# Seven block products instead of eight for a quad of weight tiles in the last FFN

## Chip, cores and metric

The kernel runs on one core of a Trainium2 chip. The metric is the device time of one execution in microseconds; the median of several runs is quoted. Five engines work side by side, each with its own in-order queue: TensorE (PE in the profile, its weight loads PEld), VectorE (DVE), ScalarE (ACT), GpSimd (POOL) and SyncE (SP, which here only issues DMAs).

## What is computed

One residual block on 256 tokens of width 2048 in float32: an FFN, a mixer (mLSTM and RG-LRU side by side), and a second FFN. The change touches the second FFN:

```python
def _swiglu(u, w13, w2):
    g, v = jnp.split(u @ w13, 2, axis=-1)
    return (jax.nn.silu(g) * v) @ w2

y = _swiglu(modulate(x, 2), ffn2_w13[l], ffn2_w2[l])
x = _layer_norm(ALPHA * x + FFN_WEIGHT * gate[:, 2, None, :] * y, ln_g[l, 2], ln_b[l, 2])
```

`w13` is 2048 x 11264 (5632 gate columns and 5632 value columns), `w2` is 5632 x 2048. `gate` comes from a product of the conditioning vector c with `w_ada`.

## The kernel before

**Precision.** A float32 product is made of three products in the PE's faster type: both operands are split into a high part `hi` and a rest `lo`, and hi*hi, hi*lo and lo*hi are summed in PSUM. For the tokens these are `uh` and `ul`. For a weight tile (128 x 2048: four chunks of 128 rows by 512 columns), `load` (line 83) fetches 1 MB into a buffer of the tag "raw" (four of them), `split` (line 90) has ACT cast it into a `hi` buffer (line 97) and DVE subtract to get `lo` (line 99); there are three buffers of each.

**The product of a tile.** `mov_t` (line 264) multiplies a tile with one half t of the tokens (128 of 256): 4 chunks x 3 matmuls (lines 271 to 273) with the tokens as stationary and 512 weight columns as moving operand, 12 matmuls in all. `mov_w` (line 296) does both halves, 24 matmuls.

**The last FFN.** The 5632 hidden columns are 11 blocks b of 512; two blocks are a group gi. `rows_block(b)` (line 648) takes 4 gate tiles and 4 value tiles (the k-th covers 512 of the 2048 input rows), and `swiglu` (line 667) makes silu(g)*v. `turn_one` (line 674) transposes such a 128 x 512 piece with four PE instructions, ACT and DVE split it into `hth` and `htl`. `g2(gi)` (line 862) multiplies a group with its 8 tiles of w2 and adds into `yacc`. The loop at the end of `ffn` runs block 0 and 1, blocks 2 and 3, g2(0), blocks 4 and 5, g2(1) and so on to blocks 8 and 9, g2(3), then `residual` (line 309) on what has been summed, block 10, and `closing` (line 897) with the last three sets of w2 tiles and the last LayerNorm.

**Work in between.** The rows of `w_ada` are reduced on DVE by `ada_tile` (line 181): a load into a raw buffer and one multiply-and-sum with `scb`, silu(c) in every partition. `tick` (line 199) is called by every load, adds `credit[1]` (here FFN2_RATE, from a start of -2) and issues an ada tile whenever a whole credit has gathered. `gate_rows` (line 206) turns the finished gate column into a row and spreads it over the partitions by DMA on POOL's queue. `scale_x` (line 318) multiplies x by ALPHA on ACT.

**What sets the order.** A planner orders each engine's instructions ahead of time by its own timing; on each engine it takes what it thinks is ready, the earlier written first, and buffers are given out as they come free. Only instructions issued through `Pinned` handles (line 113: V, A, G, T, Q) keep the written order among themselves. In the last FFN before the change the weights' products are not pinned.

Of the kernel before, what the change touches and what calls it, by code (L numbers as in the profile page):

```python
# [29 lines left out]
GRP = 8  # L30
# [8 lines left out]
RAMP_RATE = (1.0, 0.8, 1.0, 0.6)  # L39
FFN1_RATE = 0.88  # L40
MIX_RATE = 0.5
FFN2_RATE = 0.3

SLOT = 2176


@with_exitstack
def block_kernel(ctx: ExitStack, tc: tile.TileContext, a: dict, out: bass.AP):
    nc = tc.nc
# [15 lines left out]
    def bank(name):  # L65
        return psp.tile([P, 512], F32, tag="ps", name=name)
# [4 lines left out]
    def raw_tile(name):  # L71
        n_raw[0] += wide[0]
        if wide[0] and n_raw[0] % 3 == 0:
            return slot(name)[:, 0:D]
        return wp.tile([P, 2048], F32, tag="raw", bufs=4, name=name)


    credit = [0.0, 0.0]
# [34 lines left out]
    class Pinned:  # L113


        def __init__(self, engine):
            self.engine = engine
            self.last = None
# [36 lines left out]
            T.matmul(ps[:, 0:P], ident, ident, start=True, stop=True)  # L155


    scb = big.tile([P, D], F32, name="scb")
    sc = cst.tile([P, KT], F32, name="sc")
    nc.scalar.dma_start(sc, a["c"])  # L160
    nc.scalar.activation(sc, sc, AF.Silu)
# [1 line left out]
    idle(c_rows[3], 9)  # L163
    for n in range(4):
        rows_of(c_rows[n], sc[:, 4 * n:4 * n + 4])
    x = big.tile([P, NT, D], F32, name="x")


    u2 = big.tile([P, KT, 2, S], F32R, name="u2")
    uh, ul = u2[:, :, 0, :], u2[:, :, 1, :]  # L170
# [1 line left out]
    badac = cst.tile([P, 3, 3, KT], F32, name="badac")  # L172
    adac = cst.tile([P, 3, 3, KT], F32, name="adac")
    modc = adac[:, :, 0:2, :]
    gate = big.tile([P, D], F32, name="gate")
    rowd = ctx.enter_context(tc.tile_pool(name="dr", bufs=1, space=bass.MemoryType.DRAM)).tile([KT, P], F32, name="rowd")


    todo = list(enumerate(_ada_tiles()))
# [26 lines left out]
    def gate_rows(s, weight):  # L206

        ps = bank(f"adag{s}")
        nc.tensor.transpose(ps[0:KT, 0:P], adac[:, s, 2, :], ident)
        row = sm.tile([KT, P], F32, tag="grow", bufs=1, name=f"grow{s}")  # L210
        nc.scalar.mul(row, ps[0:KT, 0:P], weight)
        nc.gpsimd.dma_start(rowd, row)
        nc.gpsimd.dma_start(gate, rowd.rearrange("a b -> (a b)").rearrange("(o n) -> o n", o=1).to_broadcast([P, D]))


    def rstd_of(var, name):
# [44 lines left out]
        for k in range(KT):  # L261
            nc.tensor.matmul(ps[:, 0:S], lo[:, k * P:(k + 1) * P], uh[:, k, :], start=False, stop=k == KT - 1)  # L262

    def mov_t(ps, hl, acth, actl, k0, t, first, last):

        hi, lo = hl
        tk = slice(t * P, (t + 1) * P)
        for j in range(4):
            w = slice(j * 512, (j + 1) * 512)
            o = like(ps, hi)  # L270
            nc.tensor.matmul(o, acth[:, k0 + j, tk], cut(hi, w), start=first and j == 0, stop=False)  # L271
            nc.tensor.matmul(o, acth[:, k0 + j, tk], cut(lo, w), start=False, stop=False)  # L272
            end = nc.tensor.matmul(o, actl[:, k0 + j, tk], cut(hi, w), start=False, stop=last and j == 3)  # L273
        return end

    def mov_u(ps, hl, k, t, first, last, between=lambda: None, both=True):
# [16 lines left out]
            w = slice(j * 512, (j + 1) * 512)  # L293
            T.matmul(o, ul[:, 4 * k + j, t * P:(t + 1) * P], cut(hl[0], w), start=False, stop=last and j == 3)

    def mov_w(pss, hl, acth, actl, k0, first, last):
        for t in range(NT):
            end = mov_t(pss[t], hl, acth, actl, k0, t, first, last)
        return end

    def half(t):
# [16 lines left out]
    def scale_x():  # L318
        for t in range(NT):
            A.mul(x[:, t, :], x[:, t, :], ALPHA)  # L320
# [312 lines left out]
    def ffn(s, w13, w2, start, following=None):  # L633
# [11 lines left out]
        def new_h(gi):  # L645
            hts[gi] = [slot(f"{w}{gi}", F32R)[:, 0:GRP * S].rearrange("p (a b) -> p a b", a=GRP) for w in ("hth", "htl")]

        def rows_block(b, passed=None):

            i = 8 * (b - b0)  # L650
            if passed:
                pg, pv = passed[0], met(passed, w13[4:8], f"fv{s}")
            else:
                pg = [bank(f"fg{s}{b}{t}") for t in range(NT)]
                for k in range(4):
                    end = mov_w(pg, load_w(w13[i + k], f"fg{s}_{b}{k}"), uh, ul, k * 4, k == 0, k == 3)
                    if k in (1, 2):
                        turn_one(end)
                pv = [bank(f"fv{s}{b}{t}") for t in range(NT)]
                for k in range(4):  # L660
                    mov_w(pv, load_w(w13[i + 4 + k], f"fv{s}_{b}{k}"), uh, ul, k * 4, k == 0, k == 3)
            if 4 * b // GRP not in hts:
                new_h(4 * b // GRP)
            for t in range(NT):
                swiglu(b, t, pg[t], pv[t])

        def swiglu(b, t, g, v):

            sg = sm.tile([P, 512], F32, tag="u", bufs=2, name=f"sg{s}{b}{t}")
            nc.scalar.activation(sg, g, AF.Silu)  # L670
            nc.vector.tensor_mul(sg, sg, v)
            to_turn.append((b, t, sg))
# [261 lines left out]
        if start is not None:  # L934
            ramp(start)
            credit[:] = 0.0, FFN1_RATE
            done = 2
            g2(0)
        else:
            credit[:] = -2.0, FFN2_RATE  # L940
            rows_block(0, nxt.pop())
        for gi in range(done, len(groups)):
            g1(gi)
            if gi == 2 and not start:
                scale_x()
            if gi == len(groups) - 2:
                ada_until(s, 2, KT - 1)
                gate_rows(s, 0.5)
                credit[0] -= 2.0
            if gi == len(groups) - 1 and following:  # L950
                credit[:] = 0.0, 0.0
                g2_kept(gi - 1)
            elif gi == len(groups) - 1:
                closing(gi)
            elif gi:
                g2(gi - 1)
# [467 lines left out]
```

## Time and profile before

| | us |
|---|---|
| median of 3 runs (1895.41 to 1895.69) | 1895.65 |
| span of the profiled execution | 1893.8 |
| PE busy in it | 1880.4 |
| DVE busy | 1411.9 |
| ACT busy | 831.2 |
| POOL busy | 41.3 |
| read from HBM | 512.36 MB, 272 GB/s |

The profile is that of one execution. A matmul's end is modelled and neighbouring matmuls overlap, so the distance between two starts tells more than a duration. "Idle before" of a group names what ended the idle time of its engine. The profiled execution is 1.85 us shorter from first to last instruction than the median run; the rest lies around the instructions.

### The profile page before, as it was taken

The numbers are of one execution on the slowest core, as the hardware profiler recorded it, in microseconds if no ns is written. First come the engines' busy times: TensorE is split into PE (matmuls) and PEld (weight loads), VectorE is DVE, ScalarE is ACT, GpSimd is POOL, SyncE is SP. The second block draws the span as 40 slices with busy tenths as digits, with TensorE's granted clock in tenths as the row PEclk, the third lists the DMA queues.
The fourth block names the chain that finished last, engine by engine and source line by source line (L and its number), as shares of the span: only waits on it lengthen the run. The fifth ranks groups of instructions, "written<-read, shape, count | busy, mean of one in ns | idle before, by whom it ended". The sixth has DMA issues, their size and how long they took to land.

```text
span 1893.8 us, 21255 instructions
## 1 busy us (share of the span) xinstructions
PE 1880.4 (99%) x8591; PEld 1544.5 (82%) x8591; DVE 1411.9 (75%) x1372; ACT 831.2 (44%) x790; POOL 41.3 (2%) x65
## 2 busy tenths in 40 slices
PE   9999999999999999999999999999999999999998
PEld 6788888888888888788888887888888888888886
DVE  6899998887887977798986877556555644545666
ACT  4443444533334335756643357343434334343341
POOL 0000000000000000000000121000000000000000
PEclk9999999999999999999999999999999999999999
DMA  9989889899899886477787663666676655555562
GB/s 378 416 355 360 311 315 374 336 354 351 344 362 356 333 316 252 170 289 269 274 320 269 215 248 128 242 257 248 239 258 242 227 196 193 184 200 202 198 222 89
DMA packets 74498, 515.87 MB, mean 272 GB/s; under 512 B 8688, under 2 KB 8864, under 8 KB 13472
## 3 DMA queue, kind: packets, MB, share of 16 engines
q1 hardware_dynamic: 72144, 507.54, 71.3%
q10 hardware_dynamic: 1728, 3.80, 0.6%
q0 software_dynamic: 528, 3.17, 0.4%
q8 instruction: 67, 1.10, 0.2%
q14 instruction: 31, 0.25, 0.0%
HBM read 512.36 MB, written 2.12 MB: 272 GB/s over the span
## 4 chain that ended last, share of the span: by engine, by line
PE 94%; DVE 3%; DMA 1%; ACT 1%; issue 1%; POOL 0%; POOLq 0%; DVEq 0%; SPq 0%; ACTq 0%
PE py L272 6%; PE py L271 6%; PE py L273 6%; PE fg L272 6%; PE fg L271 6%; PE fg L273 6%; PE fv L271 6%; PE fv L272 6%; PE fv L273 6%; PE pj L260 5%; PE pj L262 3%; PE tl L271 2%; PE tl L272 2%; PE tl L273 2%; PE rv L738 2%; PE rv L739 2%
## 5 line engine op out<-in xcount | busy, mean ns | idle before, releaser
L191 DVE CUSTOM_DVE_ANT_0 ada<-ada,scb,badac 128x2048 f32<-128x2048 f32 x110 | 258.0, 2346 | 11.3 <-DMA ada<-in_w_ada 10.9
L99 DVE TENSOR_TENSOR lw<-rw,hw 128x2048 fp32r<-128x2048 f32 x81 | 185.3, 2290 | 96.2 <-ACT hw L97 96.2
L97 ACT CAST hw<-rw 128x2048 fp32r<-128x2048 f32 x81 | 155.1, 1914 | 216.9 <-PE py L273 80.8
L99 DVE TENSOR_TENSOR lfv<-rfv,hfv 128x2048 fp32r<-128x2048 f32 x60 | 137.5, 2292 | 133.9 <-ACT hfv L97 133.7
L99 DVE TENSOR_TENSOR lfg<-rfg,hfg 128x2048 fp32r<-128x2048 f32 x60 | 137.5, 2291 | 89.7 <-ACT hfg L97 89.6
L272 PE MATMUL py<-lw,hth 128*128 128x512 f32 x512 | 199.4, 389 | 0.1
L273 PE MATMUL py<-hw,htl 128*128 128x512 f32 x512 | 199.4, 389 | 0.0
L97 ACT CAST hfg<-rfg 128x2048 fp32r<-128x2048 f32 x60 | 114.9, 1914 | 191.4 <-PE fv L273 52.9
L271 PE MATMUL py<-hw,hth 128*128 128x512 f32 x512 | 197.7, 392 | 0.0
L97 ACT CAST hfv<-rfv 128x2048 fp32r<-128x2048 f32 x60 | 114.6, 1912 | 165.3 <-PE fg L273 91.7
L272 PE MATMUL fg<-lfg,u 128*128 128x512 f32 x480 | 187.0, 389 | 0.1
L273 PE MATMUL fg<-hfg,u 128*128 128x512 f32 x480 | 187.0, 389 | 0.0
L272 PE MATMUL fv<-lfv,u 128*128 128x512 f32 x480 | 186.8, 389 | 0.0
L273 PE MATMUL fv<-hfv,u 128*128 128x512 f32 x480 | 186.7, 389 | 0.0
L271 PE MATMUL fg<-hfg,u 128*128 128x512 f32 x480 | 185.0, 392 | 0.0
L271 PE MATMUL fv<-hfv,u 128*128 128x512 f32 x480 | 183.5, 389 | 0.0
L260 PE MATMUL pj<-u,hs 128*128 128x512 f32 x512 | 122.5, 391 | 0.0
L97 ACT CAST hra<-rra 128x2048 fp32r<-128x2048 f32 x38 | 72.6, 1915 | 102.8 <-DMA rra<-in_w_r 49.1
L272 PEld LDWEIGHTS py<-lw,hth 128*128 128x128 f32 x512 | 96.2, 188 | 20.4 <-DVE lw L99 0.9
L273 PEld LDWEIGHTS py<-hw,htl 128*128 128x128 f32 x512 | 96.1, 188 | 20.2
L271 PEld LDWEIGHTS py<-hw,hth 128*128 128x128 f32 x512 | 95.9, 188 | 19.3
L260 PEld LDWEIGHTS pj<-u,hs 128*128 128x128 f32 x512 | 94.3, 188 | 18.4
(472 smaller groups left out, 3552.5 us busy)
## 6 DMA issues: line engine op xcount, KB each, us to landing
ada<-in_w_ada SPq DMA_DIRECT2D x138, 1024.0 KB, 6.0
rw<-in_w SPq DMA_DIRECT2D x81, 1024.0 KB, 5.0
rfg<-in_w SPq DMA_DIRECT2D x60, 1024.0 KB, 4.8
rfv<-in_w SPq DMA_DIRECT2D x60, 1024.0 KB, 4.8
rra<-in_w_r SPq DMA_DIRECT2D x45, 1024.0 KB, 7.4
rs<-in_w_s SPq DMA_DIRECT2D x32, 1024.0 KB, 4.9
rwo<-in_w_out SPq DMA_DIRECT2D x16, 1024.0 KB, 4.8
rv<-in_w_vo SPq DMA_DIRECT2D x8, 1024.0 KB, 4.9
```

What stands on the lines that cost most here:

```text
L97: act.copy(cut(hi, w), like(raw[:, w], hi))
L99: low.tensor_sub(cut(lo, w), like(raw[:, w], lo), cut(hi, w).bitcast(F32))
L191: vec.tensor_tensor_reduce(raw[:, c], raw[:, c], scb[:, c], 1.0, base, ALU.mult, ALU.add, to)
L260: nc.tensor.matmul(ps, hi[:, k * P:(k + 1) * P], both(k), start=k == 0, stop=False)
L262: nc.tensor.matmul(ps[:, 0:S], lo[:, k * P:(k + 1) * P], uh[:, k, :], start=False, stop=k == KT - 1)
L271: nc.tensor.matmul(o, acth[:, k0 + j, tk], cut(hi, w), start=first and j == 0, stop=False)
L272: nc.tensor.matmul(o, acth[:, k0 + j, tk], cut(lo, w), start=False, stop=False)
L273: end = nc.tensor.matmul(o, actl[:, k0 + j, tk], cut(hi, w), start=False, stop=last and j == 3)
L738: pe.matmul(pss[t], uh[:, k0 + j, tk], hi[:, w], start=go, stop=False)
L739: pe.matmul(pss[t], uh[:, k0 + j, tk], lo[:, w], start=False, stop=False)
```

## The change

For blocks 2 to 9, `rows_block` and `g2` are replaced by `fast_block`. It takes the gate tiles 0 and 1 (ta, tb) and the value tiles 0 and 1 (tc_, td), a 2 x 2 quad with the token halves on the other side, by Strassen's scheme in Winograd's form: 7 calls of `mov_t` for the quad, not 8. Four of them use sums of token blocks, which `sums` makes once into `ws`; the weight sums are made in place in the raw buffers, four subtractions of a whole tile on DVE a block, and the results are split like tiles. The other four w13 tiles are multiplied as before, 8 calls. Partial results are copied out of PSUM by ACT (`kept`) and added by DVE. Four w2 tiles are written in between in each block (`x_tile`), for the group two blocks earlier. All these products go through T, so PE keeps the written order.

`ws` takes the place of x in SBUF: x goes to DRAM (`xd`) before the first of these blocks and comes back after the last. Two more raw buffers (six) replace the own places of `scb` and `gate`, which now hold one raw buffer each as long as they live. FFN2_RATE becomes 0.5. `mov_t` and `mov_w` get the engine handle as an argument. `scale_x` moves from group 2 to behind the way back of x.

The core of the diff (left out: the handle arguments, small helpers, and the loop over groups, which skips what `fast_block` has done):

```diff
-FFN2_RATE = 0.3
+FFN2_RATE = 0.5
+RAW = 6
+FAST = range(2, 10)
+class Held:
+    def __init__(self, tile):
+        self.tile = tile
+    def __getitem__(self, key):
+        return self.tile[key]
...
-        return wp.tile([P, 2048], F32, tag="raw", bufs=4, name=name)
+        return wp.tile([P, 2048], F32, tag="raw", bufs=RAW, name=name)
-    scb = big.tile([P, D], F32, name="scb")
+    scb = raw_tile("scb")
-    x = big.tile([P, NT, D], F32, name="x")
+    def tokens(name):
+        return big.tile([P, NT, D], F32, tag="x", name=name)
+    x = Held(tokens("x0"))
-    gate = big.tile([P, D], F32, name="gate")
+    gate = Held(raw_tile("gate0"))
+    xd = dr.tile([P, NT, D], F32, name="xd")
...
+        def sums():
+            nc.gpsimd.dma_start(xd, x.tile)
+            f = raw_tile("sums").rearrange("p (a b) -> p a b", b=P)
+            for t in range(NT):
+                tk = slice(t * P, (t + 1) * P)
+                nc.vector.tensor_add(f[:, 8 * t:8 * t + 8, :], uh[:, 0:8, tk].bitcast(F32), ul[:, 0:8, tk].bitcast(F32))
+            a11, a12, a21, a22 = (f[:, 4 * i:4 * i + 4, :] for i in range(4))
+            nc.vector.tensor_add(a22, a21, a22)
+            nc.vector.tensor_sub(a21, a11, a21)
+            nc.vector.tensor_sub(a11, a22, a11)
+            nc.vector.tensor_sub(a12, a12, a11)
+            both = big.tile([P, 2, KT, P], F32R, tag="x", name="ws")
+            nc.scalar.copy(both[:, 0], f)
+            nc.vector.tensor_sub(both[:, 1], f, both[:, 0].bitcast(F32))
+            return both[:, 0], both[:, 1]
+        def restore():
+            x.tile = tokens("x1")
+            for t in range(NT):
+                nc.gpsimd.dma_start(x[:, t, :], xd[:, t, :])
+            scale_x()
+        def fast_block(b, wh, wl):
...
+            u, w = (uh, ul), (wh, wl)
+            ta = fresh(0)
+            end = part(p1, halves(ta), u, 0, 0, True, True)
+            turn_one(end)
+            f1 = kept(p1, "u", "fs")
+            tc_ = fresh(4)
+            end = x_tile(0)
+            turn_one(end)
+            nc.vector.tensor_sub(ta[0], tc_[0], ta[0])
+            part(p5, halves(ta, "p"), w, s1_, 0, True, True)
+            f5 = kept(p5, "gy", "ft")
+            td = fresh(5)
+            x_tile(1)
+            nc.vector.tensor_sub(ta[0], td[0], ta[0])
+            part(p1, halves(ta, "q"), w, s2_, 0, False, True)
+            f2 = kept(p1, "gy", "fv")
+            part(p5, halves(td), w, s4_, 0, False, False)
+            x_tile(2)
+            nc.vector.tensor_sub(tc_[0], td[0], tc_[0])
+            part(p1, halves(tc_, "q"), w, s3_, 0, False, True)
+            f3 = kept(p1, "u", "fu")
+            p2, p4 = bank(f"fc{b}"), bank(f"fd{b}")
+            tb = fresh(1)
+            part(p2, halves(tb), u, 4, 0, True, False)
+            g2_ = load_w(w13[i + 2], f"fw{s}_{b}2")
+            part(p2, g2_, u, 8, 0, False, False)
+            part(p4, g2_, u, 8, 1, True, False)
+            nc.vector.tensor_sub(tb[0], tb[0], ta[0])
+            part(p4, halves(tb, "p"), u, 4, 1, False, False)
+            g3_ = load_w(w13[i + 3], f"fw{s}_{b}3")
+            part(p2, g3_, u, 12, 0, False, True)
+            part(p4, g3_, u, 12, 1, False, True)
+            nc.vector.tensor_add(f1, f1, p2)
+            nc.scalar.activation(f1, f1, AF.Silu)
+            nc.vector.tensor_add(f3, f3, p4)
+            nc.scalar.activation(f3, f3, AF.Silu)
+            x_tile(3)
+            vs = [load_w(w13[i + 4 + k], f"fw{s}_{b}{4 + k}") for k in (2, 3)]
+            for t, ps in enumerate((p5, p1)):
+                for k in range(2):
+                    part(ps, vs[k], u, 8 + 4 * k, t, False, k == 1)
...
+            for t, h, v, ps in ((0, f1, f2, p5), (1, f3, f5, p1)):
+                nc.vector.tensor_add(v, v, ps)
+                nc.vector.tensor_mul(h, h, v)
+                to_turn.append((b, t, h))
...
             rows_block(0, nxt.pop())
+            rows_block(1)
+            ws = sums()
+            for b in FAST:
+                fast_block(b, *ws)
+            restore()
+            done = FAST.stop // 2 - 1
```

In the parts left out, `fresh(k)` is a load of w13 tile k, `halves` is split on ACT and DVE, `part` is mov_t with T, `kept` copies a PSUM bank to SBUF on ACT, and `x_tile(m)` is load_w and mov_w of one w2 tile with the sum into yacc after every second one (on ACT for group 0, on DVE after that).

## Rows read from the trace of the kernel before

**Rows 1.** The page: busy time of PE, and the chain that ended last.

```profile
PE 1880.4 (99%) x8591; PEld 1544.5 (82%) x8591; DVE 1411.9 (75%) x1372; ACT 831.2 (44%) x790; POOL 41.3 (2%) x65
...
PE 94%; DVE 3%; DMA 1%; ACT 1%; issue 1%; POOL 0%; POOLq 0%; DVEq 0%; SPq 0%; ACTq 0%
```

**Rows 2.** Timeline of PE: start, duration, engine, line, operation.

```profile
1242.69 0.39 PE L271 MATMUL fg<-hfg,u 128*128 128x512 f32 x1
...
1300.08 0.39 PE L272 MATMUL fg<-lfg,u 128*128 128x512 f32 x1
...
1303.70 0.39 PE L273 MATMUL fg<-hfg,u 128*128 128x512 f32 x1
...
1315.28 0.39 PE L271 MATMUL fv<-hfv,u 128*128 128x512 f32 x1
...
1773.49 0.39 PE L271 MATMUL fg<-hfg,u 128*128 128x512 f32 x1
```

**Rows 3.** Timeline of ACT in block 3; in brackets its idle time before.

```profile
1298.23 1.91 ACT L97 CAST hfv<-rfv 128x2048 fp32r<-128x2048 f32 x1 [3.53 <-PE fg L273]
...
1304.13 1.91 ACT L97 CAST hfv<-rfv 128x2048 fp32r<-128x2048 f32 x1 [3.52 <-PE fg L273]
...
1315.48 1.91 ACT L97 CAST hfv<-rfv 128x2048 fp32r<-128x2048 f32 x1 [3.04 <-PE fv L273]
...
1320.92 1.91 ACT L97 CAST hw<-rw 128x2048 fp32r<-128x2048 f32 x1 [3.53 <-PE fv L273]
```

**Rows 4.** Stretches: length, PE, PEld, DVE, ACT, POOL busy; clock, DMA, GB/s.

```profile
1177.00:1242.70 65.70, 65.70 (x296) 54.38 (x295) 39.26 (x26) 28.17 (x20) 0.00 (x0) 1.00 0.68 253
...
1242.70:1773.50 530.80, 530.80 (x2379) 439.60 (x2378) 292.05 (x189) 208.98 (x141) 1.18 (x2) 1.00 0.60 220
...
1773.50:1817.20 43.70, 43.70 (x194) 36.23 (x193) 28.09 (x25) 18.32 (x11) 0.00 (x0) 1.00 0.55 194
...
1883.00:1893.80 10.80, 4.09 (x10) 1.43 (x8) 5.79 (x9) 0.60 (x2) 1.69 (x2) 0.87 0.41 137
...
20.00:30.00 10.00, 8.31 (x20) 3.53 (x19) 6.73 (x10) 1.72 (x3) 0.00 (x0) 1.00 1.03 410
```

**Rows 5.** Waits, blocks 2 to 9: us in total, times, longest.

```profile
ACT hfv L97 <- PE fg L273: 73.3, 24, 3.5
...
SPq L87 <- DVE lfg L99: 130.9, 28, 5.0
...
POOL rowd L212 <- ACT grow L211: 570.4, 1, 570.4
```

**Rows 6.** PE's waits over the whole span, the longest line.

```profile
PE rg L122 <- ACT u L122: 2.2, 2, 1.7
```

**Rows 7.** Groups of DVE in the mixer: xcount, busy us, mean ns.

```profile
L1127 DVE TENSOR_TENSOR ii<-ii,xc 128x2048 f32<-128x2048 f32 x1 | 2.3, 2283 | 0.0
```

**Rows 8.** Timeline of DVE in block 3.

```profile
1300.17 2.29 DVE L99 TENSOR_TENSOR lfv<-rfv,hfv 128x2048 fp32r<-128x2048 f32 x1 [3.15 <-ACT hfv L97]
1302.38 0.68 DVE L688 TENSOR_TENSOR htl<-th,hth 128x512 fp32r<-128x512 f32 x1
1302.98 2.34 DVE L191 CUSTOM_DVE_ANT_0 ada<-ada,scb,badac 128x2048 f32<-128x2048 f32 x1
...
1317.42 2.29 DVE L99 TENSOR_TENSOR lfv<-rfv,hfv 128x2048 fp32r<-128x2048 f32 x1 [3.15 <-ACT hfv L97]
```

**Rows 9.** Groups of ACT by line, blocks 2 to 9.

```profile
L877 ACT COPY yacc<-py 128x512 f32<-128x512 f32 x8 | 4.7, 589 | 11.7 <-PE py L273 11.7
...
L122 ACT ACTIVATE x<-x 128x2048 f32<-128x2048 f32 x2 | 3.7, 1910 | 0.0
```

**Rows 10.** Groups of DVE by line from 1150 us to the end.

```profile
L191 DVE CUSTOM_DVE_ANT_0 ada<-ada,scb,badac 128x2048 f32<-128x2048 f32 x16 | 37.5, 2346 | 0.9 <-DMA ada<-in_w_ada 0.9
```

**Rows 11.** DMA issues by line: queue, xcount, KB each, us to landing.

```profile
rw<-in_w SPq DMA_DIRECT2D x81, 1024.0 KB, 5.0
...
gate<-rowd POOLq DMA_DIRECT2D x3, 1024.0 KB, 6.9
```

More of the change, by code (lines that the diff above doesn't have):

```diff
@@ L174, in block_kernel @@
     modc = adac[:, :, 0:2, :]
-    gate = big.tile([P, D], F32, name="gate")
-    rowd = ctx.enter_context(tc.tile_pool(name="dr", bufs=1, space=bass.MemoryType.DRAM)).tile([KT, P], F32, name="rowd")
+    gate = Held(raw_tile("gate0"))
+    dr = ctx.enter_context(tc.tile_pool(name="dr", bufs=1, space=bass.MemoryType.DRAM))
+    rowd = dr.tile([KT, P], F32, name="rowd")
+    xd = dr.tile([P, NT, D], F32, name="xd")
     todo = list(enumerate(_ada_tiles()))
@@ L212, in gate_rows @@
         nc.gpsimd.dma_start(rowd, row)
-        nc.gpsimd.dma_start(gate, rowd.rearrange("a b -> (a b)").rearrange("(o n) -> o n", o=1).to_broadcast([P, D]))
+        if s:
+            gate.tile = raw_tile(f"gate{s}")
+        nc.gpsimd.dma_start(gate[:, :], rowd.rearrange("a b -> (a b)").rearrange("(o n) -> o n", o=1).to_broadcast([P, D]))
     def rstd_of(var, name):
@@ L262, in stat_u, with mov_t @@
             nc.tensor.matmul(ps[:, 0:S], lo[:, k * P:(k + 1) * P], uh[:, k, :], start=False, stop=k == KT - 1)
-    def mov_t(ps, hl, acth, actl, k0, t, first, last):
+    def mov_t(ps, hl, acth, actl, k0, t, first, last, pe=nc.tensor, **kw):
         hi, lo = hl
@@ L270, in mov_t @@
             o = like(ps, hi)
-            nc.tensor.matmul(o, acth[:, k0 + j, tk], cut(hi, w), start=first and j == 0, stop=False)
-            nc.tensor.matmul(o, acth[:, k0 + j, tk], cut(lo, w), start=False, stop=False)
-            end = nc.tensor.matmul(o, actl[:, k0 + j, tk], cut(hi, w), start=False, stop=last and j == 3)
+            pe.matmul(o, acth[:, k0 + j, tk], cut(hi, w), start=first and j == 0, stop=False, **kw)
+            pe.matmul(o, acth[:, k0 + j, tk], cut(lo, w), start=False, stop=False, **kw)
+            end = pe.matmul(o, actl[:, k0 + j, tk], cut(hi, w), start=False, stop=last and j == 3, **kw)
         return end
@@ L294, in mov_low, with mov_w @@
             T.matmul(o, ul[:, 4 * k + j, t * P:(t + 1) * P], cut(hl[0], w), start=False, stop=last and j == 3)
-    def mov_w(pss, hl, acth, actl, k0, first, last):
+    def mov_w(pss, hl, acth, actl, k0, first, last, pe=nc.tensor):
         for t in range(NT):
-            end = mov_t(pss[t], hl, acth, actl, k0, t, first, last)
+            end = mov_t(pss[t], hl, acth, actl, k0, t, first, last, pe)
         return end
@@ new lines, in restore, with part, fresh, halves @@
+        def restore():
[4 more added lines that the diff above has]
+        def fast_block(b, wh, wl):
+            i = 8 * b
+            gi = 4 * b // GRP - 1
+            s2_, s4_, s3_, s1_ = 0, 4, 8, 12
+            p1, p5 = bank(f"fa{b}"), bank(f"fb{b}")
+            py = {}
+            def part(ps, hl, h, k0, t, first, last):
+                return mov_t(ps, hl, *h, k0, t, first, last, T, skip_group_check=not first and ps in (p1, p5))
+            def fresh(k):
+                return load(w13[i + k], f"fw{s}_{b}{k}")
+            def halves(tile, w=""):
+                return split((tile[0], tile[1] + w, None), nc.scalar, nc.vector)
+            def kept(ps, tag, w):
+                to = sm.tile([P, 512], F32, tag=tag, bufs=2, name=f"{w}{s}{b}")
+                nc.scalar.copy(to, ps)
+                return to
+            def x_tile(m):
+                n, k = b % 2 * 2 + m // 2, m % 2
+                if not k:
+                    py[n] = [bank(f"py{gi}_{n}_{t}") for t in range(NT)]
+                kg = 2 * gi + k
+                end = mov_w(py[n], load_w(w2[kg * 4 + n], f"w2{s}_{kg}_{n}"), *hts[gi], k * 4, not k, k == 1, T)
+                if k:
+                    c = slice(n * 512, (n + 1) * 512)
+                    for t in range(NT):
+                        if gi == 0:
+                            evac.append(nc.scalar.copy(yacc[t][:, c], py[n][t]))
+                        else:
+                            nc.vector.tensor_add(yacc[t][:, c], yacc[t][:, c], py[n][t])
+                return end
+            u, w = (uh, ul), (wh, wl)
[39 more added lines that the diff above has]
+                    part(ps, vs[k], u, 8 + 4 * k, t, False, k == 1)
+            if 4 * b // GRP not in hts:
+                new_h(4 * b // GRP)
+            for t, h, v, ps in ((0, f1, f2, p5), (1, f3, f5, p1)):
+                nc.vector.tensor_add(v, v, ps)
+                nc.vector.tensor_mul(h, h, v)
+                to_turn.append((b, t, h))
@@ L941, in ffn @@
             rows_block(0, nxt.pop())
+            rows_block(1)
[4 more added lines that the diff above has]
+            done = FAST.stop // 2 - 1
         for gi in range(done, len(groups)):
-            g1(gi)
-            if gi == 2 and not start:
-                scale_x()
+            if start or gi > done:
+                g1(gi)
             if gi == len(groups) - 2:
@@ L955, in ffn @@
             elif gi:
-                g2(gi - 1)
+                if start:
+                    g2(gi - 1)
                 if gi == len(groups) - 2:
```

## Prediction

> **What bounds the kernel now.** I read the page first: PE is busy 99% of the span, DVE 75%, and the chain that ended last is PE for 94% [rows 1]. A busy PE need not be a PE at its pace, so next came the timeline of PE: in the last FFN its matmuls of 512 columns start 0.226 to 0.227 us apart without a hole (16 steps from 1300.08 to 1303.70), although each is drawn 0.39 us long [rows 2]. So the step is the price of a matmul, not its mean duration. A tile is 24 matmuls and costs 5.44 us (0.2267 each), the distance of two casts in the timeline of ACT (1315.48 to 1320.92) [rows 3]; the four transposes of one turn_one add 0.46 us (1298.23 to 1304.13 is 5.90) [rows 3].
>
> The stage that changes runs from the first matmul of block 2 (1242.69) to that of block 10 (1773.49), 530.8 us [rows 2]. [...] By price: 8 blocks with 12 tiles each are 96 x 5.44 = 522.4, 18 turns are 8.3, together 530.7. The price list is complete.
>
> The list of waits shows who follows whom: ACT waits for PE (a cast of hi needs one of three buffers), and the load queue waits for DVE to free raw buffers [rows 5]. PE itself waits for nothing there (that view has no line of it), and its longest wait of the whole run is 1.7 us [rows 6].
>
> **What is removed.** A `fast_block` holds 15 calls of mov_t on w13 (1 on p1 from u, 4 with sums of tokens, 2 + 4 for tb, g2, g3, and 4 for the last two value tiles), where rows_block holds 16; the 8 on w2 stay. One mov_t is 12 matmuls, 2.72 us. Eight blocks save 8 x 2.72 = 21.8 us. An ideal block is 23 x 2.72 + 2 x 0.46 = 63.5 us instead of 66.2.
>
> **What is added on DVE and ACT.** Per block there are 15 splits instead of 12 (the tiles ta, tc and tb go in as sums as well) and 4 subtractions of whole tiles in place. A subtraction of 128x2048 in place lasts 2283 ns in the mixer [rows 7], much like the low part of a split; back to back these take 2.21 us and 512 columns take 0.60 [rows 8]. DVE: 19 x 2.21 + 12 x 0.60 (two turns, four adds to yacc, six adds and products at the end) = 49.2 us of 63.5. ACT: 15 casts at 1.91 [rows 3], four copies out of PSUM, two Silu and two casts after turns at about 0.59 [rows 9] make about 33 us of 63.5. Neither is the bound as a sum.
>
> **The distance between the engines.** A cast starts 0.20 us after the last user of its buffer (1315.28 to 1315.48) and the low part ends 4.23 us later (1317.42 + 2.29) [rows 2, 3, 8], so 4.43 us pass from a free buffer to a usable tile. With three buffers the tile may start when the two between are used up. Now that is 2 x 5.44 = 10.9 us, 6.4 to spare. In the new order most tiles have three products between (8.2 us), but x2 follows two single products and so does g2: 5.44 us, 1.0 to spare; x0 at the head of a block has 5.9. At these three places one extra instruction of 2.21 us on DVE makes PE late by about 1.2.
>
> I laid a block end to end with these durations, PE in written order, DVE and ACT taking the first written instruction that is ready. Without ada tiles nothing is late: the yacc adds end 0.7 us before the low part of x2 can start, and tb - ta ends about 0.9 before that of g2. So the steady block takes 63.5 us.
>
> **What the ada tiles do to it.** Sixteen are left in this FFN [rows 10]. The new FFN2_RATE is 0.5 from -2: eleven loads before block 2 bring 3, then twelve loads a block bring 6 in block 2, 6 in block 3 and 1 in block 4. One costs 2.34 us of DVE [rows 8, 10] and a short read of its sum, 2.4. In blocks 2 and 3 the yacc copies run on ACT, so DVE has 46.8 + 14.4 = 61.2 us of 63.5: full. The ada tiles also pass through the raw buffers, of which scb keeps one until the last is done, while ta, tc and tb are held over half a block; the loads behind them on SP's queue come late. Laid out with 5 us for a load [rows 11] and one of them each 3.1 us (340 GB/s; the rings moved 410 from 20 to 30 us [rows 4]), PE is late at x0, x1 and g2: 4.3 to 4.6 us in block 2 and 3.0 to 4.8 in block 3, 7.6 to 9.1 together, by whether a buffer comes free 0.3 or 0.2 us after its matmul. No less than 0 can come of it (if the ada tiles are fitted into holes that hurt nobody), and an upper end is all twelve on the path, 12 x 2.4 = 29. I take 8, near the layout; it is an estimate.
>
> **What goes once.** sums() puts two adds of 1024 columns, four of 512, a cast and a low part on DVE and ACT, about 7 and 2 us; the stretch before block 2 has DVE busy 39 of 66 us [rows 4], which hides it; without cover it costs 9. The spill of x is 2 MB on POOL's queue, where 1 MB landed in 6.9 us [rows 11], so about 14 us; POOL is empty for 570 us before its next work [rows 5], and x is final before this stage, so I set it at nothing; uncovered, the cast into ws waits in ACT's queue with the casts of the weights behind it, up to 14 us. The way back is 2 x 1 MB after the last sum product of block 9, with 33 us of PE work in that block and 43.7 in block 10 [rows 4] before the closing tiles. Its readers are scale_x on ACT (two of 1.91 [rows 9]) and the residual on DVE. If scale_x stands in ACT's queue before the data has landed, the casts behind it wait too: 0 to 6 us, once. I take 0. The adds of the residual, 16 x 0.60 = 10 us [rows 8], fit into block 10, where DVE works 28 of 43.7 us now [rows 4], a part of it this very residual.
>
> **Sum.** 21.8 - 8 = 13.8 us off the profiled span of 1893.8, so 1880.0. The median of the runs is 1895.65, 1.85 above the span; with that I forecast **1882 us**.
>
> **Rivals.**
> - *Nothing comes back.* The ada tiles fit. For it: DVE still has 2 us a block, and PE's path never waited for DVE here [rows 5]. Against: the holes are shorter than one ada tile. 1895.65 - 21.8 = 1874.
> - *A tight tile in every block.* The planner fixes DVE's order beforehand; if it puts one of the four subtractions or two short adds before x2 or g2, PE is late by 0.7 to 1.2 us once or twice in each of the six later blocks: 4 to 14 us more, 1887 to 1896.
> - *ACT held by x.* scale_x waits at the end: 3 to 6 us more, 1885 to 1888. POOL's 1 MB took 6.9 us against 5.0 on SP's queue [rows 11], which is for it; against it, ACT has half its time free.
> - *Slower.* DVE becomes the pacemaker of the fast blocks: a 2.21 us instruction ahead at all three tight places in each block costs 3 x 1.2 = 3.6 us a block, 29 in all; with the 8 of the ada tiles 1895.65 - 21.8 + 37 = 1911. It decides from 2.7 us of lateness a block (21.8 / 8). For it: 19 long instructions a block on one in-order queue. Against: 14 us a block are free after block 4.
> [...]
>
> **Chances.** Forecast 0.50 (1877 to 1886), nothing back 0.17, tight tile in every block 0.15, ACT held 0.08, slower 0.06, clock 0.04. The range reaches from 1873 to 1893: it leaves out slower (0.06), the upper third of the tight tiles (0.05), half of the clock case (0.02) and a margin under "nothing back" (0.04), together 0.17. A measurement here can tell some 0.2%, 3.8 us, from no change. Faster by more (below 1891.9): 0.50 + 0.17 + 0.08 and half of the 0.15 make 0.82. The rest of the tight tiles and the clock case give 0.09 within it, and 0.09 is left for slower, with a little for spills that are not covered.
>
> **What would show it.** In the profile after: mov_t matmuls fewer by 96 in the stage; steps of 63.5 us from block to block from block 5 on; waits of PE for DVE low parts or ACT casts in blocks 2 and 3 alone, at x0, x1 and g2, about 8 us in sum; no wait of ACT's scale_x for DMA over 2 us; clock 1.00. Wrong would be: waits of PE of over 1 us in each block (the order on DVE), a wait at the first product with ws in block 2 (the spill), or a granted clock below 1.00 in the stage.

## The result: the stage gained 17 us, the mixer and the start lost 20

| | before | after |
|---|---|---|
| median of 20 runs each, us | 1895.82 (1894.77 to 1898.14) | 1898.82 (1894.99 to 1900.50) |
| ratio | | 1.0014, 95% interval 1.0008 to 1.0021 |
| span of the profiled execution, us | 1893.8 | 1896.6 |

The forecast was 1882 us in a range of 1873 to 1893. The time lies 17 us above the forecast and outside the range; it is a loss of 0.14%, less than the 0.2% that the prediction named as the least difference to be told from none, though the whole interval lies above 1.

The page of the changed kernel: the span, the busy time of PE and DVE, the granted clock in 40 slices, and the shares of the chain that ended last.

```profile
span 1896.6 us, 21239 instructions
PE 1864.0 (98%) x8495; PEld 1527.8 (81%) x8495; DVE 1562.4 (82%) x1467; ACT 895.8 (47%) x847; POOL 41.0 (2%) x68
PEclk9999999999999999999899999999999999999999
PE 92%; DVE 4%; ACT 2%; DMA 1%; issue 1%; POOL 0%; POOLq 0%; DVEq 0%; ACTq 0%
```

PE does 96 matmuls fewer (8591 before) and is busy 16.4 us less (1880.4 before), yet the span is 2.8 us longer. So PE now stands idle where it did not; one slice of the clock, the twentieth, is below full, and it lies around 925 us, far ahead of the changed stage. The timeline of PE gives milestones (start, duration, engine, line, operation, out<-in): the last rv product at the opening, the first pj and the last pv product in the mixer, the head of block 2 and that of block 10.

```profile
298.28 0.39 PE L868 MATMUL rv<-hra,u 128*128 128x512 f32 x1
...
818.52 0.39 PE L280 MATMUL pj<-u,hs 128*128 128x512 f32 x1
...
975.48 0.39 PE L293 MATMUL pv<-hv,u 128*128 128x512 f32 x1
...
1262.73 0.39 PE L135 MATMUL fa<-hfw,u 128*128 128x512 f32 x1
...
1775.21 0.39 PE L291 MATMUL fg<-hfg,u 128*128 128x512 f32 x1
```

The same for the kernel before; its block 2 and block 10 stand in [rows 2].

```profile
295.24 0.39 PE L740 MATMUL rv<-hra,u 128*128 128x512 f32 x1
...
815.40 0.39 PE L260 MATMUL pj<-u,hs 128*128 128x512 f32 x1
...
955.40 0.39 PE L273 MATMUL pv<-hv,u 128*128 128x512 f32 x1
```

Differences of these starts, before and after, say where the time went:

| stretch | before | after | change |
|---|---|---|---|
| start to the last rv | 295.24 | 298.28 | +3.0 |
| last rv to the first pj | 520.16 | 520.24 | +0.1 |
| first pj to the last pv (mixer) | 140.00 | 156.96 | +17.0 |
| last pv to block 2 | 287.29 | 287.25 | 0.0 |
| block 2 to block 10 (the stage) | 530.80 | 512.48 | -18.3 |
| block 10 to the end of the span | 120.31 | 121.39 | +1.1 |

Two turns (0.92 us by the price of [rows 3]) now run in block 10 and not in the stage, so the stage is worth 17.4 us; the forecast said 13.8. What ate it lies in two stretches of which the prediction says nothing.

**Inside the stage.** The windows of blocks 2, 3 and 5 and of the whole stage; the columns are the window, its length, and the busy us (instructions) of PE, PEld, DVE, ACT and POOL, then granted clock, DMA share, GB/s.

```profile
1262.70:1328.70 66.00, 64.00 (x285) 52.40 (x284) 58.95 (x39) 35.04 (x27) 0.00 (x0) 1.00 0.74 287
1328.70:1394.10 65.40, 64.41 (x287) 52.41 (x286) 59.44 (x39) 35.04 (x27) 0.00 (x0) 1.00 0.74 289
1457.60:1521.10 63.50, 63.50 (x286) 52.59 (x285) 50.50 (x32) 32.76 (x23) 0.00 (x0) 1.00 0.55 199
1262.70:1775.20 512.50, 509.51 (x2274) 420.29 (x2273) 419.95 (x265) 270.27 (x195) 2.21 (x4) 1.00 0.61 228
```

From block 4 on every block takes 63.5 us with PE busy throughout; DVE works 50.5 of it (laid out: 49.2) and ACT 32.8 (laid out: 33). Blocks 2 and 3 are late by 2.6 and 1.8 us (66.04 and 65.30 against 63.49). The timeline of PE has the two longest of their waits, in brackets with what ended them:

```profile
1298.92 0.50 PE L135 MATMUL fc<-lfw,u 128*128 128x512 f32 x1 [1.50 <-DVE lfw L112]
...
1342.16 0.50 PE L135 MATMUL py<-lw,hth 128*128 128x512 f32 x1 [0.77 <-DVE lw L112]
```

The first is g2 in block 2, the second x1 in block 3: two of the three places (x0, x1, g2) where the layout of the prediction had PE late with the ada tiles; x0 is not late. The other two waits of the stage, 0.5 and 0.2 us, are at turns.

**In the mixer.** Here `proj` ends with the last pj, `rg_out` (lines 1266 to 1278) makes rh and rl for the RG-LRU branch on ACT and DVE, and PE goes on with the products pv of eight tiles of `w_vo` (line 1297). The timeline of PE after:

```profile
924.83 1.22 PE L291 MATMUL pv<-hv,u 128*128 128x512 f32 x2 [10.08 <-ACT hv L110]
929.09 0.80 PE L292 MATMUL pv<-lv,u 128*128 128x512 f32 x1 [3.04 <-DVE lv L112]
929.68 0.63 PE L293 MATMUL pv<-hv,u 128*128 128x512 f32 x1
930.11 0.63 PE L291 MATMUL pv<-hv,u 128*128 128x512 f32 x1
...
932.74 0.40 PE L292 MATMUL pv<-lv,u 128*128 128x512 f32 x1
932.97 0.40 PE L293 MATMUL pv<-hv,u 128*128 128x512 f32 x1
```

PE waits 10.08 us for the first high part of `w_vo`, then 3.04 us for its low part. What ACT does meanwhile, in its timeline after:

```profile
915.05 0.25 ACT L229 ACTIVATE grow<-adag 16x128 f32<-16x128 f32 x1
921.81 1.17 ACT L1277 CAST rh<-t 128x512 fp32r<-128x512 f32 x2 [6.51 <-DVE t L1276]
922.88 1.89 ACT L110 CAST hv<-rv 128x2048 fp32r<-128x2048 f32 x1
```

ACT's queue holds two casts to rh ahead of the first cast of a `w_vo` tile. They wait 6.51 us for DVE, and the cast of the weights stands behind them. In the kernel before, two tiles of `w_vo` are cast and a third is begun before PE asks for the first (at 911.39):

```profile
903.21 1.91 ACT L97 CAST hv<-rv 128x2048 fp32r<-128x2048 f32 x1
...
906.18 1.91 ACT L97 CAST hv<-rv 128x2048 fp32r<-128x2048 f32 x1
...
909.65 1.92 ACT L97 CAST hv<-rv 128x2048 fp32r<-128x2048 f32 x1 [1.20 <-PE pj L260]
```

There the first cast to rh comes at 934.83. The instructions are the same, their order on ACT is not: the planner has turned round two pieces of work that the diff does not touch. The experiments ask what made it do so.

**At the start.** The list of waits of the first 100 us, PE alone (us in total, times, longest), and the issues on SP's queue:

```profile
PE rg L135 <- ACT u L135: 4.1, 1, 4.1
...
8.30 6.74 SPq L205 DMA_DIRECT2D ada<-in_w_ada  x6
15.46 2.20 SPq L882 DMA_DIRECT2D rra<-in_w_r  x2
```

Before, SP issues four loads of ada tiles there and the next weights at 13.35; now a fifth raw buffer is free, six loads of half an ada tile go ahead, and DVE waits 2.36 us for one of them behind which u is made. PE then does four products of the opening at a lower clock; its timeline after, and the same before:

```profile
28.33 3.38 PE L135 MATMUL rg<-rra,u 128*128 128x512 f32 x4 [4.11 <-ACT u L135]
```

```profile
25.82 1.98 PE L122 MATMUL rg<-rra,u 128*128 128x512 f32 x4 [1.69 <-ACT u L122]
```

Behind the wait of 4.11 us the granted clock from 28 to 32 us is 0.60 (before: 1.00), and the four products last 3.38 us, not 1.98. So 1.4 of the 3.0 us are the clock.

### The profile page after: what moved, and what is told of

The parts are those of the page before. It is cut to its first block, busy times and chain, and to the rows that moved or that the text cites. A ratio compares the mean times of both kernels' runs of the same rounds, so it can differ in the third digit from the quotient of the medians.

```text
span 1896.6 us, 21239 instructions
## 1 busy us (share of the span) xinstructions
PE 1864.0 (98%) x8495; PEld 1527.8 (81%) x8495; DVE 1562.4 (82%) x1467; ACT 895.8 (47%) x847; POOL 41.0 (2%) x68
## 4 chain that ended last, share of the span: by engine, by line
PE 92%; DVE 4%; ACT 2%; DMA 1%; issue 1%; POOL 0%; POOLq 0%; DVEq 0%; ACTq 0%
PE py L135 9%; PE pj L280 5%; PE fa L135 5%; PE fb L135 4%; PE fd L135 3%; PE fc L135 3%; PE py L292 3%; PE py L291 3%; PE py L293 3%; PE pj L282 3%; PE fg L292 3%; PE fg L293 3%; PE fg L291 3%; PE fv L293 2%; PE fv L291 2%; PE fv L292 2%
## 5 line engine op out<-in xcount | busy, mean ns | idle before, releaser
L112 DVE TENSOR_TENSOR lfw<-rfw,hfw 128x2048 fp32r<-128x2048 f32 x56 | 128.2, 2290 | 28.3 <-ACT hfw L110 28.1
L110 ACT CAST hfw<-rfw 128x2048 fp32r<-128x2048 f32 x56 | 107.3, 1915 | 58.6 <-PE py L135 28.2
L110 ACT CAST hs<-rs 128x2048 fp32r<-128x2048 f32 x32 | 61.1, 1909 | 83.9 <-PE pj L280 69.0
L110 ACT CAST hfg<-rfg 128x2048 fp32r<-128x2048 f32 x28 | 53.6, 1915 | 82.4 <-DMA rfg<-in_w 51.6
L112 DVE TENSOR_TENSOR lfv<-rfv,hfv 128x2048 fp32r<-128x2048 f32 x28 | 64.1, 2289 | 30.5 <-ACT hfv L110 30.2
L292 PE MATMUL fg<-lfg,u 128*128 128x512 f32 x224 | 87.4, 390 | 0.1
L293 PE MATMUL fg<-hfg,u 128*128 128x512 f32 x224 | 87.3, 390 | 0.0
L292 PE MATMUL fv<-lfv,u 128*128 128x512 f32 x224 | 87.2, 389 | 0.0
L293 PE MATMUL fv<-hfv,u 128*128 128x512 f32 x224 | 87.1, 389 | 0.0
L112 DVE TENSOR_TENSOR ls<-rs,hs 128x2048 fp32r<-128x2048 f32 x32 | 73.1, 2283 | 17.0 <-ACT hs L110 17.0
```

The lines of the kernel that those rows point to most:

```text
L110: act.copy(cut(hi, w), like(raw[:, w], hi))
L112: low.tensor_sub(cut(lo, w), like(raw[:, w], lo), cut(hi, w).bitcast(F32))
L292: pe.matmul(o, acth[:, k0 + j, tk], cut(lo, w), start=False, stop=False, **kw)
L293: end = pe.matmul(o, actl[:, k0 + j, tk], cut(hi, w), start=False, stop=last and j == 3, **kw)
```

## Experiments

Theory: the changed raw buffers (six, with `scb` and the gate among them) cost the 20 us outside the stage, and the products in the stage do what was forecast. Rivals: the stage's own work reaches back into the mixer (its loads are planned there); or the clock, which falls in the hole (0.50 from 919 to 931 us), makes up a good part of the loss.

**1. The buffers alone.** The kernel before, with nothing but the change of the raw buffers; and three ways of leaving it out of the full change.

```diff
-        return wp.tile([P, 2048], F32, tag="raw", bufs=4, name=name)
+        return wp.tile([P, 2048], F32, tag="raw", bufs=6, name=name)
-    scb = big.tile([P, D], F32, name="scb")
+    scb = raw_tile("scb")
-    gate = big.tile([P, D], F32, name="gate")
+    gate = Held(raw_tile("gate0"))
...
+        if s:
+            gate.tile = raw_tile(f"gate{s}")
```

> The kernel before with the change of the raw buffers alone: six buffers of the tag raw, scb and gate in two of them, gate taken anew for each of the three gates. No fast blocks, FFN2_RATE as before, x where it was. Theory P (the pool): the profile after lost 3.1 us in the first 30 us and 16.9 us at the first v product of the mixer, both ahead of the fast blocks, because the planner, given a fifth free raw buffer there, queues the loads and the casts in another order. Then this kernel is slower than before by about 20 us, 1915 us, with a wait of PE of about 10 us ahead of pv. Rival F (the fast blocks, FFN2_RATE or the spill shift the planner's order everywhere): this kernel stays at 1896 us and has no such wait.

Measured: 1923.58 us, ratio 1.0144 (1.0128 to 1.0159). The start is 4.2 us longer, and first pj to last pv takes 157.0 us (819.65 to 976.65), as in the changed kernel; PE's wait for the first high part is 10.09 us. 7 us more, which no expectation had, are lost between 1750.10 and 1762.68, behind the making of the last FFN's gate, which is taken anew too. The timeline of PE there, and the window after the waits:

```profile
1752.52 0.73 PE L282 MATMUL py<-hw,hth 128*128 128x512 f32 x2 [2.15 <-ACT hw L106]
1754.85 0.79 PE L283 MATMUL py<-lw,hth 128*128 128x512 f32 x1 [1.59 <-DVE lw L108]
...
1756.00:1760.00 4.00, 4.00 (x11) 3.13 (x10) 3.19 (x2) 0.07 (x1) 0.00 (x0) 0.50 1.00 340
```

The waits are 3.7 us; the other 3.3 are matmuls 0.43 us apart at a grant of 0.50. So the buffers by themselves do all of the damage outside the stage, with none of the seven products; the stage's own work is not needed for it.

**2. The gate keeps its buffer in the mixer.** In the changed kernel the mixer's gate is written into the buffer of the first one:

```diff
-        if s:
+        if s == 2:
```

> The changed kernel, with the second gate written into the first gate's buffer (a new one is taken for the third gate alone), so that the mixer has four free raw buffers as before. Theory P: the 10 us wait ahead of pv and the slow clock behind it go, 16.9 us; the first 30 us, where gate has not been written yet and five buffers are free, keep their 3.1 us. 1898.8 - 16.9 = 1882 us. Rival F: the wait stays, 1899 us.

Measured: 1881.37 us, ratio 0.9922 (0.9907 to 0.9937). First pj to last pv takes 140.1 us (818.95 to 959.02), as before the change: the 17 us are gone. The start keeps its loss (last rv at 298.75). The order of ACT's casts at the head of pv is that of the kernel before. This one condition turns the change from a loss of 3.0 us into a gain of 14.5.

**3. The buffer held from the beginning.** As in 2, and a small write claims the gate's buffer at the start, so that four are free there as before:

```diff
+    nc.gpsimd.memset(gate[:, 0:8], 0.0)
```

> As e2_gate_kept, and eight columns of the first gate's buffer are cleared at the very start, so that the buffer is taken from then on and four are free as before. Theory P: the first 30 us are as before too, another 3.1 us: 1879 us, with first waits as in the kernel before. If the start is slower by the two runs' chance alone, 1882 us as e2_gate_kept. Rival F: 1896 to 1899 us.

Measured: 1878.55 us, ratio 0.9907 (0.9892 to 0.9922). The last rv comes at 295.60 and the mixer takes 140.07. The timeline of PE at the head of pv, and of ACT at the first cast to rh:

```profile
912.02 0.48 PE L292 MATMUL pv<-hv,u 128*128 128x512 f32 x1
...
935.48 0.62 ACT L1278 CAST rh<-t 128x512 fp32r<-128x512 f32 x1 [2.22 <-DVE t L1277]
```

The order on ACT is again that of the kernel before, and the hole of 10 us is gone. The gain, 17.3 us off the median, is what the stage gives (17.4).

**4. Own places for scb and the gate, four raw buffers.** The full change without any change of the buffers:

```diff
-RAW = 6
+RAW = 4
-    scb = raw_tile("scb")
+    scb = big.tile([P, D], F32, name="scb")
-    gate = Held(raw_tile("gate0"))
+    gate = Held(big.tile([P, D], F32, name="gate"))
-        if s:
-            gate.tile = raw_tile(f"gate{s}")
```

> The changed kernel with four raw buffers and scb and gate in places of their own, as before; fast blocks, spill of x and FFN2_RATE as changed. Theory P: start and mixer as before, nothing lost there. In the fast blocks ta, tc and td or tb hold three of four buffers, so the loads come one at a time: a wait of PE in each block, somewhere between 2.7 us (then it equals before, 1896 us) and 10 us (1896 - 22 + 80 = 1954 us). If it comes out below 1885 us, the two more buffers were not needed and the 20 us were paid for nothing. Rival F: as after, 1899 us or more.

Measured: 1900.47 us, ratio 1.0028 (1.0017 to 1.0038). The start and the mixer are as before (295.32; 140.0), but blocks 2 and 3 take 73.4 and 78.3 us, and blocks 4 and 5 64.0 each. The list of waits in the stage, PE alone:

```profile
PE py L135 <- ACT hw L110: 11.5, 2, 7.6
PE py L135 <- DVE lw L112: 6.9, 7, 1.5
PE fc L135 <- DVE lfw L112: 0.6, 2, 0.3
```

Twice PE waits for the high part of a w2 tile whose load came late: by the code ta, tb and tc are held over half a block, and the ada tiles pass through the same four buffers. The expectation had a wait in every block; blocks 6 to 9, where no ada tile is left, take 63.49 us with four buffers too. So the two more buffers are needed in the stage where ada tiles pass (against blocks of 63.49 the changed kernel loses 4.4 us there, this one 25.7), and ahead of it the changed buffers do harm.

**5. No ada tiles in the last FFN.** As in 3, and the 16 ada tiles of the last FFN are left out, its gate being a constant:

```diff
+            todo.clear()
+            nc.gpsimd.memset(adac[:, 2, 2, :], 0.25)
```

> e3_gate_held with the sixteen ada tiles of the last FFN left out (their loads and their reductions; the third gate is then a constant). Theory A (the ada tiles make blocks 2 and 3 late, as the prediction had it): the steps of blocks 2 and 3, 66.0 and 65.3 us in the profile after, become 63.5 like the others, and the time falls by the 4.4 us that they are over: 1878.6 - 4.4 = 1874 us. Rival S (the way into the fast blocks makes them late: the token sums, the spill, the turns of block 1): they stay over, 1878 us.

Measured: 1873.75 us, ratio 0.9881 (0.9866 to 0.9896). PE has no wait in the stage; the blocks take 63.5 us each, and block 2 to block 10 is 508.1 us (1242.66 to 1750.76). Against 530.80, less the 0.92 of the two turns, that is 21.8 us: the saving of the prediction, 8 x 2.72, to the tenth. In experiment 3 the same stretch is 512.2, so the ada tiles cost 4.1 us there.

**6. The ada tiles spread.** As in 3, with them spread over the whole FFN:

```diff
-FFN2_RATE = 0.5
+FFN2_RATE = 0.17
```

> e3_gate_held with FFN2_RATE 0.17 for 0.5, so that the sixteen ada tiles come about two to a block, to the end of the stage. Theory A with DVE as the scarce thing: a block has 49 + 5 us of DVE work in 63.5, so hardly a wait is left: 1875 to 1877 us. If the place of an ada tile counts and not their number in a block (each may fall ahead of a tile with 1 us to spare), as much or more is lost as now: 1879 to 1884 us.

Measured: 1875.91 us, ratio 0.9893 (0.9879 to 0.9906). The waits of PE in the stage:

```profile
PE fa L135 <- DVE lfw_40q L112: 1.3, 1, 1.3
PE py L135 <- DVE lw L112: 0.2, 1, 0.2
```

Of the kernels that compute everything this is the fastest measured: 20.4 us below the kernel before on the same chip. The rate of 0.5 packs twelve ada tiles into two blocks (DVE 58.95 and 59.44 us of some 65.5); spread out, they cost 2.5 us of the stage (510.65 us, against 508.1 without them) and not 4.1.

**7. PE kept busy in the hole.** The changed kernel, with 60 matmuls of the identity written between the last pj and the first pv, so that the clock does not fall while everything else stays:

```diff
+        projected = proj(9, 8, gg, {3: rg_gates, 5: recurrence})
...
+        with tc.issue_after(projected.ins):
+            idle(bank("warm1"), 60)
```

> The changed kernel as it is, with 60 matmuls of 128 columns on the identity put into the wait of PE ahead of pv (some 7 of its 10 us; nobody reads them). It asks what share of the 16.9 us lost there is the clock. After the wait ten matmuls start 0.43 us apart and not 0.227, which is 2.0 us, and the wait for the low part of the first v tile follows DVE whatever the clock is. Theory W (the wait is the loss, the clock little): granted clock 1.00 there, 1898.8 - 2 = 1897 us. Rival C (the clock is a large part): 1890 to 1893 us.

Measured: 1899.28 us, ratio 1.0015 (1.0006 to 1.0025). The windows of the mixer, first the changed kernel (columns as above):

```profile
915.00:919.00 4.00, 0.00 (x0) 0.00 (x0) 4.00 (x4) 0.30 (x2) 1.14 (x2) 0.95 0.09 23
919.00:923.00 4.00, 0.00 (x0) 0.00 (x0) 3.86 (x5) 1.19 (x3) 0.00 (x0) 0.50 0.60 242
923.00:927.00 4.00, 1.22 (x2) 0.50 (x2) 4.00 (x9) 2.45 (x3) 0.00 (x0) 0.50 0.00 0
927.00:931.00 4.00, 1.91 (x5) 1.53 (x6) 4.00 (x3) 0.55 (x1) 0.00 (x0) 0.50 0.21 45
931.00:935.00 4.00, 4.00 (x16) 3.23 (x15) 3.40 (x6) 1.86 (x2) 0.11 (x1) 0.84 0.93 365
```

then the one with the added matmuls:

```profile
916.00:920.00 4.00, 4.00 (x38) 4.00 (x36) 4.00 (x5) 0.62 (x2) 1.14 (x2) 1.00 0.03 6
924.00:928.00 4.00, 4.00 (x38) 4.00 (x37) 4.00 (x8) 2.45 (x3) 0.00 (x0) 1.00 0.03 14
932.00:936.00 4.00, 4.00 (x18) 3.03 (x17) 3.89 (x6) 1.37 (x2) 0.11 (x1) 1.00 0.95 352
```

In the changed kernel the grant falls to 0.50 while PE stands idle, and stays there for the first products, whose starts are 0.43 us apart (929.68 to 930.11) and 0.23 again from 932.74. With the added matmuls it is 1.00 throughout, yet first pj to last pv takes 156.98 us (820.03 to 977.01), against 156.96 without them. The 2 us that the expectation gave back did not come. The timeline of PE in the changed kernel shows why:

```profile
937.95 0.50 PE L292 MATMUL pv<-lv,u 128*128 128x512 f32 x1 [1.59 <-DVE lv L112]
```

Behind the first tile PE waits for DVE's low part of the second, and gets it 119.4 us after the first pj in both kernels (937.95 and 939.44). What the full clock gains on the first tile ends in this wait. So the low clock costs nothing in the mixer beyond the hole.

**8. Four buffers and spread ada tiles.** As in 4, with FFN2_RATE at 0.17: does spreading do what the two more buffers do?

```diff
-FFN2_RATE = 0.5
+FFN2_RATE = 0.17
```

> e4_own_places (four raw buffers, scb and gate in their own places) with FFN2_RATE 0.17. In e4 the blocks with six ada tiles took 70.6 and 78.3 us, those without 63.5 to 64.0. Theory R (an ada tile in one of four raw buffers holds up a load wherever it falls, 1 to 2 us each): sixteen of them cost 16 to 32 us as before, 1890 to 1906 us. Theory A (six in a block are too many, two are not): 1876 to 1880 us, and the change of the raw buffers was not needed.

Measured: 1909.70 us, ratio 1.0071 (1.0057 to 1.0084), above even theory R's range. (The 70.6 us of the expectation is 73.4 for block 2 of experiment 4.) Blocks 2 to 4 take 66.9, 65.8 and 65.3 us, the next four 68.2 each and block 9 73.3: with four buffers the ada tiles cost PE time wherever they pass, and spread out they cost more (544.1 us for the stage, 533.8 in experiment 4). Spreading helps only when the buffers are there.

**9. Fewer added matmuls.** As in 7 with 38, to fill the hole and not delay the first pv, since the 60 ended only at 929.39:

```diff
-            idle(bank("warm1"), 60)
+            idle(bank("warm1"), 38)
```

> e7_kept_busy with 38 matmuls on the identity in place of 60. In e7 those took 13.3 us and so put off the first v product by 3 us; its granted clock stayed 1.00 and the median was that of the changed kernel. 38 take 8.4 us and fit into the wait. Theory W (the wait is the loss): the first v product comes as late after the last projection as in the changed kernel, 10.3 us later than before, the clock stays 1.00, and the products after it gain what the half rate cost there, 2 us by the ten matmuls at 0.43 us: the mixer is slower than before by about 15 us, not 17. Rival C (the clock is a large part): the mixer is slower by 11 to 13 us. The start of the kernel varies by some us from run to run, so the stretch from the last projection to the last v product in the profile decides.

Measured: 1896.58 us, ratio 1.0003 (0.9994 to 1.0012). The added matmuls end at 920.16, and the clock falls all the same after them (0.51 and 0.63 in the two stretches from 923 to 931). First pj to last pv is 156.98 us (815.71 to 972.69), and PE again gets the second low part 119.4 us after the first pj (935.15). Three times the same length, with the clock high, low and in between; neither theory's figure, 15 us or 11 to 13, came. What this run gained against 7 it gained at the start (last rv at 295.49), with the same six loads issued there. The grant stayed at 1.00 there behind a wait of 2.89 us, and the four products took 1.98 us; in experiment 7 the wait was 4.13, the grant 0.50 and the four products took 3.78.

**10. Five raw buffers.** The changed kernel, with four buffers free in the mixer as before, but the gate taken anew there. This sets apart two readings of experiment 2, which changed both:

```diff
-RAW = 6
+RAW = 5
```

> The changed kernel with five raw buffers in place of six: scb and the gate in them as in the change, the gate taken anew for each gate. So four are free at the start and in the mixer, as in the kernel before. Theory one (the fifth free buffer lets the mixer's order go another way): the distance from the first pj matmul to the last pv matmul is 140.0 us as before, without the hole of 10 us behind the first pv; start within 0.5 us of before. Theory two (the gate taken anew in the mixer does it): the distance stays at 157.0 with the hole. By both, blocks 2 and 3 are about as late as with the own places and four buffers (73.4 and 78.3 us, 20 us above the changed kernel), so the time is about 1898.8 - 3 - 17 + 20 = 1899 by theory one and about 1916 by theory two.

Measured: 1944.18 us, ratio 1.0258 (1.0241 to 1.0275). The timeline of ACT and that of PE at the head of pv:

```profile
947.30 1.16 ACT L1277 CAST rh<-t 128x512 fp32r<-128x512 f32 x2 [6.86 <-DVE t L1276]
948.37 1.90 ACT L110 CAST hv<-rv 128x2048 fp32r<-128x2048 f32 x1
...
950.32 1.22 PE L291 MATMUL pv<-hv,u 128*128 128x512 f32 x2 [10.65 <-ACT hv L110]
```

The hole is there, and first pj to last pv takes 157.5 us (843.43 to 1000.98). So it is the gate taken anew from the raw buffers in the mixer, not the fifth free one. Once the gate is taken, this run has three buffers left for the loads there, the changed kernel four as before; the hole is the same, so their number does not make it. The stage is as late as forecast (533.5 us; blocks 2 and 3 take 74.2 and 77.8). Two of my numbers missed: the start lost 5.7 us and not 0.5, and the first FFN lost 22 us, on which I had not counted. There the gate's own raw buffer would leave three for the loads where the kernel before has four; that this is the cause was not tested.

**What stays open.** Why a new buffer for the gate makes the planner put the casts to rh ahead of those of `w_vo` is in no trace: the loads of the mixer stand in the same order on SP's queue, and only ACT's and DVE's work is turned round. Some of these loads go out later (the third of `w_vo` at 906.61, before at 896.49), but the first, issued at 884.09, landed 5.0 us after that, so its cast at 922.88 did not wait for data. The start is settled in part: with six half ada tiles ahead the loss was 3.0, 4.2, 3.5, 4.2 and 0.25 us (the changed kernel, experiments 1, 2, 7 and 9). In the first four the grant from 28 to 32 us was 0.50 to 0.60, in experiment 9 it was 1.00, so the fall of the clock makes up much of the difference. With four ahead the loss was -0.5 to 0.4 in experiments 3 to 6 and 8, but 5.7 in experiment 10. There 1.8 us were lost by 81 us, with the grant at 0.81 and 0.76 from 32 to 40, and the rest later; it was not followed up.

## Why the prediction was wrong, step by step

- **What is removed: right.** 21.8 us were forecast, and 21.8 came when nothing was late (experiment 5).
- **Steady block, DVE and ACT: right.** 63.5 us a block; DVE 50.5 for 49.2, ACT 32.8 for 33. The tight tile in every block did not come, nor DVE as pacemaker: from block 4 on PE's wait is none.
- **Blocks 2 and 3: the right mechanism, its size too large.** The term was 8 us; it measured 4.4 (2.6 and 1.8), and 4.1 by the difference of experiments 3 and 5. Of the three places that the layout had late, x0 never was: the layout had put an ada tile ahead of it. The case "nothing back" (1874) is what experiment 5 gives (1873.75) once the ada tiles are gone.
- **Spill, sums and way back: right.** In the table of issues the 2 MB spill landed after 11.0 us (forecast 14) and the two halves that come back after 5.7 and 9.0; block 2 starts without a wait of ACT for it. scale_x starts on ACT as soon as the cast ahead of it ends:

```profile
1759.13 1.91 ACT L110 CAST hfw<-rfw 128x2048 fp32r<-128x2048 f32 x1
1760.95 3.71 ACT L135 ACTIVATE x<-x 128x2048 f32<-128x2048 f32 x2
```

- **The clock: right in the stage, where it is 1.00 in every window shown.** It fell in the mixer, to 0.50, where the prediction looked for no fall, and cost nothing there by itself (experiments 7 and 9). It also fell at the start, where it is 1.4 of the 3.0 us lost. The chances put 0.04 on a fall of the clock, half of it beyond the range; no run shows a loss of that size by the clock (11 us, from 1882 to 1893). In its place the runs showed matmuls that start 0.43 us apart at a grant of 0.50, and not 0.227: from 929.68 to 932.24 in the mixer, and from 1755.44 to 1760.56 in experiment 1, where it cost 3.3 us. In the stage of experiment 4, with four buffers and a longest wait of 7.6 us, the grant was 0.95 and 0.93 over blocks 2 and 3. PE's longest wait in the kernel before is 1.7 us [rows 6]; for waits of some 3 us the start has two cases. In experiment 2 the grant fell to 0.50 behind a wait of 3.07 us, and four products took 3.78 us for 1.98; in experiment 9, behind 2.89 us, it stayed at 1.00.
- **The step that failed: what was not in the sum.** "Two more raw buffers (six) replace the own places of scb and gate" was told as a part of the change and given no price, not even from both sides. I read the change as one of blocks 2 to 9 and took the 1243 us ahead of them as they were. But the raw buffers serve every load of the kernel, and the planner gives them out as they come free; the text ahead of the prediction says itself that it orders each engine by its own timing. So a change of the buffers can reorder any stage. It did: 17.0 us in the mixer by the gate taken anew (experiments 2 and 10), and 3.0 at the start with six loads ahead for four, in part by the clock. Without these 20 the time would have been 1878.55 (experiment 3), in the range and 3.5 us under the forecast.
- **Signs that were in the profile.** In the mixer ACT is not far ahead of PE: in the kernel before, the first cast of a `w_vo` tile starts at 903.21, and PE wants the tile at 911.39. Two casts of rh that wait 6.51 us for DVE, set ahead of it, were enough. A case "the buffers reorder another stage" would have had its place among the rivals; no row of before gives its price, but with some 10 us or more the range would have reached over 1895.

## What to carry on

A change of a pool that the whole kernel shares belongs in the sum for every stage that draws on it, not only for the stage that wanted it; where a planner sets the order, compare the order on each engine in all stages before looking at the stage that was rewritten. When a large saving moves the time little, line up a few milestones of the busiest engine, before and after: the lost time stands between two of them. And give a long-lived tile its buffer once (here one condition and one small write were worth 20 us), since each new request is a point at which the order can turn.

## What the runs showed of the hardware

- What a grant of 0.50 cost hung on the next wait. In the mixer it cost nothing: 157.0 us from the first pj to the last pv at 0.50 (the changed kernel), at 1.00 (experiment 7) and in between (0.51 and 0.63, experiment 9), because PE had to wait for DVE's next low part anyway (1.59, 1.59 and 1.43 us). At the start (0.60 from 28 to 32 us), and behind the last gate of experiment 1 (0.50), no such wait followed, and it cost 1.4 and 3.3 us.
- The 60 matmuls of the identity, 128 columns of float32, took 13.3 us (916.10 to 929.39; the trace has two records for each), 0.22 us each, the price of one matmul of 512 columns in the faster type (0.227).
- 2 MB from SBUF to DRAM on POOL's queue landed in 11.0 us. The same 2 MB the other way, as two transfers of 1 MB issued 0.6 us apart, landed 5.7 and 9.0 us after their issue, 9.6 us in all.
